# Second SwiGLU of a hybrid decoder layer: a fourth Strassen piece in the down products, with weight sums of two pieces made early and kept in DRAM

## The chip, the cores and the metric

The kernel runs on one core of a Trainium2 chip. The core has a matrix engine (TensorE, "PE" in the profile; its weight loads are listed apart as "PEld"), three engines for element-wise work (VectorE "DVE", ScalarE "ACT", GpSimd "POOL") and a synchronisation engine ("SP") that here only issues DMA transfers. Data lives in DRAM, in the on-chip memory SBUF, and, for results of TensorE, in eight PSUM banks. The metric is the time of one execution on the device in microseconds (us).

## The reference

One decoder layer for 256 positions of 1024 channels in float32. Three sub-layers follow each other, each between two RMS norms and added to the stream `h`. The first and the last are SwiGLUs with 2816 inner channels, the middle one is a mixer (a state-space branch and a differential attention, merged by gates).

```python
def rmsnorm(x, g):
    y = xf * lax.rsqrt(jnp.mean(xf * xf, axis=-1, keepdims=True) + EPS)
    return y.astype(x.dtype) * g

def swiglu(x, w_gate, w_up, w_down):
    return (jax.nn.silu(x @ w_gate) * (x @ w_up)) @ w_down
...
h = h + 0.5 * rmsnorm(swiglu(rmsnorm(h, ffn1_pre_g[l]), ffn1_w_gate[l], ffn1_w_up[l], ffn1_w_down[l]),
                      ffn1_post_g[l])
u = rmsnorm(h, mix_pre_g[l])
...
h = h + rmsnorm(merged @ w_out[l], mix_post_g[l])
h = h + 0.5 * rmsnorm(swiglu(rmsnorm(h, ffn2_pre_g[l]), ffn2_w_gate[l], ffn2_w_up[l], ffn2_w_down[l]),
                      ffn2_post_g[l])
```

The last SwiGLU is called f2 here, the first f1.

## The kernel before

**Splits.** A float32 product is made of three matmuls in the type fp32r. Each operand is split in a high half, which ScalarE makes by a cast, and a low half, which VectorE makes by subtracting the high half from the source. The three terms are high x high, low x high and high x low. For weights the halves are called `whi` and `wlo` (L271, L272), for the products of gate and up `gh` and `gl` (L332, L333).

**Weights.** All weights come in chunks of 1 MB, listed in `chunks` in the order of their use. `load_to` (L244) issues the loads on SP's queue, three raw buffers deep (`RAW_BUFS`). `split_steps` (L256) splits a chunk in two rows of 128x1024 on each engine, and `split_to` (L300) keeps the splits three chunks ahead of the matmuls. The halves live in a pool `k4` of 29 buffers of 4 KB a partition, which also holds the activations. When both halves of a chunk are made, its raw buffer is given to the next chunk.

**Gate and up.** The inner channels are cut into 11 pieces of T = 256. Pieces 0 and 1 are made first, by `pn_f` products with the positions on the partitions: the result is transposed (L978) and split from the PSUM tile `pt_f`. For pieces 2 to 10 `ffn` (L957) loops over `j`: gate chunk (`pg_f`), ScalarE's Silu, up chunk (`pup_f`), VectorE's product `sg` (L997), split into `gh` and `gl`. In the bank of a gate or up result the high and the low terms lie apart; ScalarE copies one (L359) and VectorE adds the other (L360), giving `sg` and `su`.

**Down.** The plan is a string, `DOWN` (L49), for both SwiGLUs "q1 p q2 p q3 ppp". A `p` is one piece of T: 24 matmuls of 128x512 and one weight chunk, so two low halves. A `qN` is a Strassen piece over pieces 2N and 2N+1: seven products p1 to p7 in place of eight, 42 matmuls in place of 48. Its operands are, beside quarters of the weights, four sums of quarters, made by VectorE (`wt`, L123) from the two raw chunks just before they are used, and four sums of the activations, made in `sums_of` (L743) while gate and up still run. Each of the seven weight operands is split by `Quad.split`: ScalarE `wqh` (L131), VectorE `wql` (L137). The products are taken in the order `FIRST` = 1, 2, 3, 5, 7, 6, 4, in the last Strassen piece in the order `LAST` = 1, 6, 7, 2, 3, 5, 4.

`mm_quads` (L834) takes the Strassen pieces and the plain ones between them, all added up in eight PSUM banks (L844), and `combine` (L869 to L872) puts the Strassen banks together. `mm_n` (L664, matmuls at L688) adds the remaining plain pieces and ends in the norm.

**Order.** Through most of f2 the order of the rows on each engine is set by the framework's scheduler, which works with its own costs and with the pools; each engine then executes its rows strictly in that order. A row that waits holds up all rows behind it on its engine. In the names below a number behind a tile's name is a counter: `wlo1050` is the low half 0 of chunk 105, `wql1145` the low half of product p5 of the Strassen piece that starts with chunk 114. In f2 chunks 93 to 110 are gate and up of pieces 2 to 10, in turns, and the down weights begin with chunk 111.

The functions that the change touches, with the loop over gate and up in `ffn`, follow.

## Time and profile before

| | |
|---|---|
| time, median of 3 runs | 728.9 us (728.49 to 729.12) |
| the profiled execution's own time | 728.89 us |
| its span | 727.2 us |
| TensorE busy | 719.8 us (99%), 4019 instructions |
| VectorE busy | 621.1 us (85%), 950 instructions |
| ScalarE busy | 478.8 us (66%), 816 instructions |
| GpSimd busy | 31.3 us (4%), 63 instructions |
| DMA | 137.93 MB, mean 190 GB/s |

The span goes from the first to the last recorded instruction; the profiled execution's time is 1.7 us longer. On the span's clock, f2's first products (`pn_f`) run from 541 to 564.6 us, gate and up from 564.6 to 665.2, the 174 matmuls of `mm_quads` from 665.2 to 704.6, the plain pieces behind them to 719.7; then come the last matmuls, the norm and the store.

How to read it: "L353 PE" is TensorE's work from line 353 of the kernel. A group's line gives busy time and mean duration, and behind them the engine's idle time ahead of its rows with the instruction that ended it ("<-ACT whi" means a cast on ScalarE was waited for). In lists of an engine's rows in time the first two columns are start and length in us. In a table of stretches the columns are the stretch, its length, and the busy times of PE, PEld, DVE, ACT and POOL, each with the number of rows, then the granted clock, the share of DMA time and the rate in GB/s. VectorE's rows overlap a little: a row of 128x1024 shows 1.22 us, and the next begins before it ends.

### The profile page before, as it was taken

The page shows a single profiled execution, that of the slowest core. Times are in us where ns is not written, and L with a number is a line of the kernel's source. Part 1 is how long each engine was busy: PE and PEld are TensorE (multiplying, and loading weights), DVE is VectorE, ACT ScalarE, POOL GpSimd, SP SyncE. Part 2 cuts the span into 40 slices and gives each one's busy share as a digit, 9 for nine tenths or more (in the row PEclk, how much of TensorE's full clock was granted, in tenths as well). Part 3 has the DMA queues.
Part 4 walks back from the last instruction along what each step waited for, and adds up shares of the span by engine and source line. Part 5 has one row for each costly group of instructions (what it writes and reads, how often), then busy time and mean ns, then how long its engine had stood idle before and what let it go on. Part 6 is the DMA issues. An engine that isn't in the chain of part 4 may idle for free.

```text
span 727.2 us, 10595 instructions
## 1 busy us (share of the span) xinstructions
PE 719.8 (99%) x4019; PEld 619.7 (85%) x4019; DVE 621.1 (85%) x950; ACT 478.8 (66%) x816; POOL 31.3 (4%) x63
## 2 busy tenths in 40 slices
PE   9999999999999999999999999999999999999996
PEld 8888888888878889999888788888888888888885
DVE  6978788999979999777996998789786878789996
ACT  5657566666867676969975577774664757576562
POOL 4300000000200000000000000000011000000000
PEclk9999999999999999999999999999999999999999
DMA  8874655567673557666564663474543654654551
GB/s 299 235 267 148 222 162 185 174 229 260 185 232 118 181 167 225 202 200 215 150 224 150 203 222 132 165 234 169 169 153 116 232 189 161 230 196 152 181 195 58
DMA packets 94452, 137.93 MB, mean 190 GB/s; under 512 B 2669, under 2 KB 68801, under 8 KB 94401
## 3 DMA queue, kind: packets, MB, share of 16 engines
q1 hardware_dynamic: 91728, 129.51, 54.4%
q0 software_dynamic: 2368, 7.22, 3.4%
q8 instruction: 31, 0.51, 0.3%
q10 hardware_dynamic: 304, 0.53, 0.2%
q14 instruction: 21, 0.16, 0.1%
HBM read 136.17 MB, written 1.08 MB: 189 GB/s over the span
## 4 chain that ended last, share of the span: by engine, by line
PE 91%; DVE 4%; ACT 2%; issue 1%; DMA 1%; DVEq 0%; ACTq 0%
PE pup_f L353 14%; PE pg_f L353 14%; PE pxs L353 6%; PE pws L394 6%; PE pgt L394 6%; PE acc_f2p L844 5%; PE pbc L353 3%; PE pk L353 3%; PE pq L353 3%; PE pwd L394 3%; PE pn_f L410 3%; PE pn_f L394 3%; PE acc_f1p L844 3%; PE pn_mx L394 2%; PE acc_f2p L688 2%; PE pz L345 2%
## 5 line engine op out<-in xcount | busy, mean ns | idle before, releaser
L272 DVE TENSOR_TENSOR wlo<-raw,whi 128x1024 fp32r<-128x1024 f32 x212 | 252.2, 1219 | 18.3 <-ACT whi L271 17.9
L271 ACT CAST whi<-raw 128x1024 fp32r<-128x1024 f32 x212 | 214.1, 1048 | 14.1 <-DMA raw<-in_w_in_dram 5.6
L353 PE MATMUL pg_f<-u_f,whi 128*128 128x512 f32 x288 | 69.0, 390 | 0.0
L353 PE MATMUL pup_f<-u_f,whi 128*128 128x512 f32 x288 | 68.7, 391 | 0.0
L353 PEld LDWEIGHTS pg_f<-u_f,whi 128*128 128x128 f32 x288 | 53.9, 188 | 11.1
L353 PEld LDWEIGHTS pup_f<-u_f,whi 128*128 128x128 f32 x288 | 52.9, 188 | 10.2
L131 ACT CAST wqh<-wt 128x1024 fp32r<-128x1024 f32 x24 | 25.2, 1054 | 23.2 <-DVE wt L123 22.0
L353 PEld LDWEIGHTS pg_f<-u_f,wlo 128*128 128x128 f32 x288 | 36.9, 191 | 1.4
L353 PE MATMUL pup_f<-u_f,wlo 128*128 128x256 f32 x288 | 37.5, 283 | 0.0
L353 PE MATMUL pg_f<-u_f,wlo 128*128 128x256 f32 x288 | 37.4, 283 | 0.0
L359 ACT COPY su_f<-pup_f 128x256 f32<-128x256 f32 x36 | 13.2, 373 | 35.9 <-PE pup_f L353 35.9
L353 PEld LDWEIGHTS pup_f<-u_f,wlo 128*128 128x128 f32 x288 | 35.9, 192 | 0.0
L360 DVE TENSOR_TENSOR su_f<-pup_f,su_f 128x256 f32<-128x256 f32 x36 | 15.2, 422 | 24.0 <-ACT su_f L359 23.9
L394 PE MATMUL pgt<-whi,u_mx 128*128 128x512 f32 x128 | 33.1, 393 | 0.0
L343 PE MATMUL pz<-u_mx,whi 128*128 128x256 f32 x128 | 31.6, 284 | 0.0
L342 PE MATMUL pz<-u_mx,whi 128*128 128x256 f32 x128 | 31.6, 284 | 0.0
L353 PE MATMUL pxs<-u_mx,whi 128*128 128x512 f32 x128 | 29.9, 390 | 0.0
L137 DVE TENSOR_TENSOR wql<-wt,wqh 128x1024 fp32r<-128x1024 f32 x24 | 29.1, 1219 | 0.2
L137 DVE TENSOR_TENSOR wql<-raw,wqh 128x1024 fp32r<-128x1024 f32 x21 | 25.4, 1219 | 3.4 <-ACT wqh L131 3.4
L394 PEld LDWEIGHTS pgt<-whi,u_mx 128*128 128x128 f32 x128 | 23.6, 188 | 5.3 <-issue 0.7
L353 PEld LDWEIGHTS pxs<-u_mx,whi 128*128 128x128 f32 x128 | 23.8, 188 | 4.8
L332 ACT CAST gh_f<-sg_f 128x512 fp32r<-128x512 f32 x18 | 11.2, 620 | 23.2 <-DVE sg_f L997 20.3
(487 smaller groups left out, 1607.7 us busy)
## 6 DMA issues: line engine op xcount, KB each, us to landing
raw<-in_w_in_dram SPq DMA_DIRECT2D x40, 1024.0 KB, 5.2
raw<-in_ffn_w_down_dram SPq DMA_DIRECT2D x22, 1024.0 KB, 4.9
raw<-in_ffn_w_gate_dram SPq DMA_DIRECT2D x20, 1024.0 KB, 5.4
raw<-in_ffn_w_up_dram SPq DMA_DIRECT2D x20, 1024.0 KB, 5.2
raw<-in_ssd_w_branch_dram SPq DMA_DIRECT2D x8, 1024.0 KB, 5.0
acb<-acd POOLq DMA_DIRECT2D x8, 512.0 KB, 4.7
raw<-in_da_w_branch_dram SPq DMA_DIRECT2D x4, 1024.0 KB, 5.8
raw<-in_w_out_dram SPq DMA_DIRECT2D x4, 1024.0 KB, 4.9
```

Source lines behind the costliest of these rows:

```text
L131: nc.scalar.copy(hi, src)
L137: nc.vector.tensor_sub(lo, src, hi.bitcast(F32))
L271: last_cast[0] = behind(nc.scalar.copy(hi, r[:, js, :]), "cast").ins
L272: m = nc.vector.tensor_sub(lo, r[:, js, :], hi.bitcast(F32))
L342: nc.tensor.matmul(acc[m], wh(j)[:, cs], ah(k0 + j), start=first and j == ks[0], stop=False)
L343: nc.tensor.matmul(acc[m], wh(j)[:, cs], al(k0 + j), start=False, stop=False)
L345: nc.tensor.matmul(acc[m], wl(j)[:, cs], ah(k0 + j), start=False, stop=last and j == ks[-1])
L353: nc.tensor.matmul(to, w_(j)[:, m * P:(m + 1) * P], x_(j), start=first and j == 0, stop=not first and j == KD - 1, skip_group_check=True)
L360: nc.vector.tensor_tensor(dst, acc[:, :T], dst, ALU.add)
L394: nc.tensor.matmul(acc, a(k0 + j), b(j), start=first and i == 0, stop=last and i == 11)
L410: nc.tensor.matmul(accs[b], x_(k0 + j), w_(j), start=first and j == 0 and w_ is wh and x_ is acts[b][0], stop=last and j == 3 and w_ is wl)
L844: nc.tensor.matmul(bank[p], x_, w_, start=p not in begun, stop=last and p in (1, 5, 6, 7))
```

## The change

- f2's plan becomes "q1 Q2 q3 Q0 ppp": the two plain pieces between the Strassen pieces (pieces 0 and 1) become a fourth Strassen piece, 0, which is now the last one and has the order `LAST`. f1's plan stays.
- `Q` is a Strassen piece with stored sums (class `Stored`). While gate and up run, `stored_sums` loads the four quarters of the piece's weights (`ws`) on GpSimd's queue into four buffers of `k4`, makes the four sums on VectorE in the same buffers, and stores each to a DRAM tile `sums_f2...` on GpSimd's queue. `ffn` steps it at fixed pieces `j`: first the job of Q2, then that of Q0. In the down products the sums come back as chunks like others, on SP's queue, so that `Stored.split` has no sums to make. For Q2 and Q0 together the down products now load eight chunks: per piece half a chunk for p1, one for p2 and p3, and two with sums.
- The chunks with sums go into the pool `u8`, whose two buffers hold the normed activations until gate and up have read them. `refill` replaces the plain call of `load_to` where a raw buffer is given back, and keeps the two kinds of buffer apart; `opened` lets the sums' loads begin only when `mm_quads` is built.
- The activations of pieces 0 and 1 are needed unsplit for piece 0's sums, so ScalarE also copies `pt_f` (`first`, two rows of 128x512), and `sums_of(0)` runs at the end of the loop's first turn. In `sums_of`, groups 0 and 3 take one split of 128x1024 in buffers of `k4` where there were one of 128x768 in `k3` and one of 128x256; this touches f1's and the mixer's too.
- `begin` in `mm_n` becomes a list of the banks not begun before it.

```diff
-DOWN = {"f1": "q1 p q2 p q3 ppp", "f2": "q1 p q2 p q3 ppp"}
+DOWN = {"f1": "q1 p q2 p q3 ppp", "f2": "q1 Q2 q3 Q0 ppp"}
...
-                    load_to(self.i + j + 1 + RAW_BUFS)
+                    refill()
...
+    class Stored(Quad):
+        def __init__(self, i, products, at):
+            self.i, self.products, self.at = i, products, at
+            self.uses = [[p for p in products if at[p][0] == n] for n in range(4)]
+        def split(self, p):
+            n, part = self.at[p]
+            load_to(self.i + n + 1)
+            src = part(raws[self.i + n])
+            hi, lo = (k4([P, 2, 512], f"wq{x_}{self.i}{p}", F32R) for x_ in "hl")
+            nc.scalar.copy(hi, src)
+            nc.vector.tensor_sub(lo, src, hi.bitcast(F32))
+            self.uses[n].remove(p)
+            if not self.uses[n]:
+                raws[self.i + n] = None
+                refill()
+            return lambda kt: hi[:, kt, :], lambda kt: lo[:, kt, :]
...
+    def stored_quad(w, k0, products, tag):
+
+        n, first = len(units), len(chunks)
+        sums = products[1:3] + products[5:] if products[1] == 6 else products[3:]
+        store = dram.tile([P, 4, D], F32, name=f"sums_{tag}{k0}")
...
+            if p == 1:
+                chunk(w[k0:k0 + 2 * P, :512].rearrange("(j p) c -> p j c", p=P), [P, 2, 512])
+                at[1] = (i, lambda r: r)
+            elif p == 2:
+                n_chunk(w, k0 + 2 * P)
+                at[2], at[3] = (i, lambda r: r[:, :, :512]), (i, lambda r: r[:, :, 512:])
+            else:
+                j = sums.index(p)
+                homes[len(chunks)] = tag
+                chunk(store[:, j:j + 2, :], [P, 2, D])
+                for o in range(2):
+                    at[sums[j + o]] = (i, lambda r, o=o: r[:, o, :].rearrange("p (k c) -> p k c", k=2))
+        del units[n:]
+        q = Stored(first, products, at)
+        units.extend((q, p) for p in products)
+        return w, k0, sums, store
...
+    def stored_sums(w, k0, sums, store):
+        t = [k4([P, 2, 512], f"ws{k0}{n}") for n in range(4)]
+        for n in (1, 0, 3, 2):
+            rows = w[k0 + n // 2 * 2 * P:k0 + (n // 2 + 1) * 2 * P, n % 2 * 512:(n % 2 + 1) * 512]
+            nc.gpsimd.dma_start(t[n], rows.rearrange("(k p) c -> p k c", p=P))
+        yield
+        for p, n, a, b in ((5, 0, 1, 0), (7, 1, 3, 1), (6, 3, 3, 0), (4, 2, 2, 3)):
+            nc.vector.tensor_sub(t[n], t[a], t[b])
+            nc.gpsimd.dma_start(store[:, sums.index(p), :], t[n].rearrange("p k c -> p (k c)"))
+            yield
...
+            elif kind == "Q":
+                stored.setdefault(tag, []).append(stored_quad(wd[0], j * 2 * T, products, tag))
...
+    def refill():
+        while len(raws) < len(chunks):
+            at_home = lambda i: (homes.get(i) is None) == (homes.get(len(raws)) is None)
+            if sum(r is not None and at_home(i) for i, r in enumerate(raws)) >= (2 if len(raws) in homes else RAW_BUFS):
+                break
+            if len(raws) in homes and homes[len(raws)] not in opened:
+                break
+            load_to(len(raws) + 1)
...
+            if i in homes:
+                if homes[i] not in opened:
+                    return
+                r = sb.tile([P, 4, 2, T], F32, tag="u8", name=f"raw{i}", bufs=2)
+                r = r.rearrange("p (a b) c t -> p a (b c t)", a=2)
+            else:
+                r = sb.tile(shape, F32, tag="raw", name=f"raw{i}", bufs=RAW_BUFS)
...
+                                             (b, q) in begin and i == 0 and kt == 0 and x_ is ah and w_ is wh,
...
+        full = g in (0, 3)
+        hi, lo = ((k4 if full else k3)([P, 4 if full else 3, 2, P], f"s{n}{g}", F32R) for n in "hl")
+        more = None if full else k2([P, 2, 2, P], f"s4{g}", F32R)
...
+        if full:
+            split(hi, lo, v)
+            return tuple([x_[:, i] for i in range(4)] for x_ in (hi, lo))
...
+        opened.add(tag)
+        refill()
...
+            if 0 in QUADS[tag]:
+                nc.scalar.copy(first[0][:, :, bs], pt_)
...
+        first = [k4([P, 4, T], f"g0_{tag}")] if 0 in QUADS[tag] else []
...
+        jobs = [stored_sums(*job) for job in stored.get(tag, ())]
+        def store_sums(at):
+            for i in at:
+                if i < len(jobs):
+                    next(jobs[i])
...
+            store_sums({4: (0,), 6: (0,), 8: (1,)}.get(j, ()))
...
+            if first:
+                sums[0] = sums_of(0, first[0][:, :2, :], first[0][:, 2:, :])
+                del first[0]
+            store_sums({2: (0,), 4: (0, 0), 5: (1,), 6: (1, 1), 8: (1,)}.get(j, ()))
```

The matmuls in `mm_quads` are 168 in place of 174; in the new kernel their line is L927. On GpSimd's queue 16 transfers stand where there was none: four loads, four stores, twice.

**Gate and up, VectorE.** Before, around the product of piece 6 (`sg_f26` by `su_f26`):

```order
L272 TENSOR_TENSOR wlo1040_6209<-raw104_6050,whi1040_6208 128x1024
L272 TENSOR_TENSOR wlo1041_6213<-raw104_6050,whi1041_6212 128x1024
L360 TENSOR_TENSOR su_f26_6207<-pup_f260_6218,su_f26_6207 128x256
L360 TENSOR_TENSOR su_f26_6207<-pup_f261_6219,su_f26_6207 128x256
L997 TENSOR_TENSOR sg_f26_6157<-su_f26_6207,sg_f26_6157 128x512
L333 TENSOR_TENSOR gl_f26_6156<-sg_f26_6157,gh_f26_6155 128x512
L272 TENSOR_TENSOR wlo1050_6261<-raw105_6100,whi1050_6260 128x1024
L272 TENSOR_TENSOR wlo1051_6265<-raw105_6100,whi1051_6264 128x1024
L272 TENSOR_TENSOR wlo1060_6311<-raw106_6166,whi1060_6310 128x1024
L360 TENSOR_TENSOR sg_f27_6259<-pg_f270_6270,sg_f27_6259 128x256
L360 TENSOR_TENSOR sg_f27_6259<-pg_f271_6271,sg_f27_6259 128x256
L272 TENSOR_TENSOR wlo1061_6315<-raw106_6166,whi1061_6314 128x1024
```

Now, at the same product; `ws0n` are the quarters, and then the sums, of Strassen piece 0:

```order
L437 TENSOR_TENSOR su_f26_6239<-pup_f260_6250,su_f26_6239 128x256
L349 TENSOR_TENSOR wlo1040_6241<-raw104_6072,whi1040_6240 128x1024
L349 TENSOR_TENSOR wlo1041_6245<-raw104_6072,whi1041_6244 128x1024
L437 TENSOR_TENSOR su_f26_6239<-pup_f261_6251,su_f26_6239 128x256
L222 TENSOR_TENSOR ws01_6178<-ws03_6180,ws01_6178 128x1024
L1093 TENSOR_TENSOR sg_f26_6187<-su_f26_6239,sg_f26_6187 128x512
L437 TENSOR_TENSOR sg_f27_6295<-pg_f270_6306,sg_f27_6295 128x256
L437 TENSOR_TENSOR sg_f27_6295<-pg_f271_6307,sg_f27_6295 128x256
L410 TENSOR_TENSOR gl_f26_6186<-sg_f26_6187,gh_f26_6185 128x512
L222 TENSOR_TENSOR ws03_6180<-ws03_6180,ws00_6177 128x1024
L349 TENSOR_TENSOR wlo1050_6297<-raw105_6122,whi1050_6296 128x1024
L349 TENSOR_TENSOR wlo1051_6301<-raw105_6122,whi1051_6300 128x1024
```

Two sums (rows of L222) stand among the rows of piece 6, the gate's additions of piece 7 (`sg_f27`) come before the low halves of chunk 105, and `gl_f26` no longer stands right behind the product.

**Gate and up, ScalarE.** Before, around the casts of the last gate chunk (109):

```order
L271 CAST whi1080_6426<-raw108_6268 128x1024
L271 CAST whi1081_6430<-raw108_6268 128x1024
L427 ACTIVATE sg_f28_6375<-sg_f28_6375 128x512
L359 COPY su_f28_6425<-pup_f280_6436 128x256
L359 COPY su_f28_6425<-pup_f281_6437 128x256
L332 CAST gh_f28_6373<-sg_f28_6375 128x512
L271 CAST whi1090_6478<-raw109_6318 128x1024
L271 CAST whi1091_6482<-raw109_6318 128x1024
L271 CAST whi1100_6528<-raw110_6384 128x1024
L359 COPY sg_f29_6477<-pg_f290_6488 128x256
L359 COPY sg_f29_6477<-pg_f291_6489 128x256
L271 CAST whi1101_6532<-raw110_6384 128x1024
```

Now:

```order
L436 COPY su_f28_6460<-pup_f280_6471 128x256
L348 CAST whi1070_6409<-raw107_6248 128x1024
L348 CAST whi1071_6413<-raw107_6248 128x1024
L436 COPY su_f28_6460<-pup_f281_6472 128x256
L348 CAST whi1080_6461<-raw108_6304 128x1024
L348 CAST whi1081_6465<-raw108_6304 128x1024
L436 COPY sg_f29_6514<-pg_f290_6525 128x256
L436 COPY sg_f29_6514<-pg_f291_6526 128x256
L409 CAST gh_f28_6406<-sg_f28_6408 128x512
L504 ACTIVATE sg_f29_6514<-sg_f29_6514 128x512
L348 CAST whi1090_6515<-raw109_6354 128x1024
L348 CAST whi1091_6519<-raw109_6354 128x1024
```

The casts of chunk 107 and 108 have moved back, behind the first copy of `su_f28`; those of chunk 109 stand behind the copies of the gate bank of piece 9 (`sg_f29`) and its Silu, where they stood ahead of them.

**Down products, TensorE.** Before, at the products p5 and p7 of Strassen piece 2 (`sh2`, `sl2` are its activation sums):

```order
L844 MATMUL acc_f2p5_6716<-wqh1145_6754,sh2_6144 128x512
L844 MATMUL acc_f2p5_6716<-wqh1145_6754,sl2_6145 128x512
L844 MATMUL acc_f2p5_6716<-wql1145_6758,sh2_6144 128x512
L844 MATMUL acc_f2p5_6716<-wqh1145_6754,sh2_6144 128x512
L844 MATMUL acc_f2p5_6716<-wqh1145_6754,sl2_6145 128x512
L844 MATMUL acc_f2p5_6716<-wql1145_6758,sh2_6144 128x512
L844 MATMUL acc_f2p7_6721<-wqh1147_6768,sh2_6144 128x512
L844 MATMUL acc_f2p7_6721<-wqh1147_6768,sl2_6145 128x512
L844 MATMUL acc_f2p7_6721<-wql1147_6772,sh2_6144 128x512
L844 MATMUL acc_f2p7_6721<-wqh1147_6768,sh2_6144 128x512
```

Now, at p5 and p7 of Strassen piece 3, which follows Q2 directly:

```order
L927 MATMUL acc_f2p5_6745<-wqh1175_6837,sh3_6398 128x512
L927 MATMUL acc_f2p5_6745<-wqh1175_6837,sl3_6399 128x512
L927 MATMUL acc_f2p7_6750<-wqh1177_6853,sh3_6398 128x512
L927 MATMUL acc_f2p5_6745<-wql1175_6841,sh3_6398 128x512
L927 MATMUL acc_f2p5_6745<-wqh1175_6837,sh3_6398 128x512
L927 MATMUL acc_f2p5_6745<-wqh1175_6837,sl3_6399 128x512
L927 MATMUL acc_f2p5_6745<-wql1175_6841,sh3_6398 128x512
L927 MATMUL acc_f2p7_6750<-wqh1177_6853,sl3_6399 128x512
L927 MATMUL acc_f2p6_6749<-wqh1176_6865,sh3_6398 128x512
L927 MATMUL acc_f2p7_6750<-wql1177_6857,sh3_6398 128x512
L927 MATMUL acc_f2p7_6750<-wqh1177_6853,sh3_6398 128x512
L927 MATMUL acc_f2p7_6750<-wqh1177_6853,sl3_6399 128x512
```

Before, p5's six matmuls were all ahead of p7's, as in the code; in the new kernel, at this piece, p7's first row stands between p5's second and third, and a matmul of p6 between p7's.

**Down products, SP.** Before, the loads of the last nine chunks:

```order
L253 DMA raw113_6536<-in_ffn2_w_down_dram 128x2x1024
L253 DMA raw114_6602<-in_ffn2_w_down_dram 128x2x1024
L253 DMA raw115_6656<-in_ffn2_w_down_dram 128x2x1024
L253 DMA raw116_6670<-in_ffn2_w_down_dram 128x2x1024
L253 DMA raw117_6760<-in_ffn2_w_down_dram 128x2x1024
L253 DMA raw118_6786<-in_ffn2_w_down_dram 128x2x1024
L253 DMA raw119_6812<-in_ffn2_w_down_dram 128x2x1024
L253 DMA raw120_6858<-in_ffn2_w_down_dram 128x2x1024
L253 DMA raw121_6892<-in_ffn2_w_down_dram 128x2x1024
```

Now the loads from the first half chunk of Q2 to the end of Q0:

```order
L330 DMA raw113_6573<-in_ffn2_w_down_dram 128x2x512
L330 DMA raw115_6751<-sums_f21024_66 128x2048
L330 DMA raw114_6639<-in_ffn2_w_down_dram 128x2x1024
L330 DMA raw116_6753<-sums_f21024_66 128x2048
L330 DMA raw117_6755<-in_ffn2_w_down_dram 128x2x1024
L330 DMA raw118_6757<-in_ffn2_w_down_dram 128x2x1024
L330 DMA raw119_6767<-in_ffn2_w_down_dram 128x2x512
L330 DMA raw120_6777<-sums_f20_67 128x2048
L330 DMA raw122_6845<-sums_f20_67 128x2048
L330 DMA raw121_6843<-in_ffn2_w_down_dram 128x2x1024
```

The first sums of Q2 (chunk 115) are loaded ahead of its chunk 114, and in Q0 the second sums (122) ahead of chunk 121.

More of the change, by code (lines that the diff above doesn't have):

```diff
@@ L877, in combine @@
             add(c4, bank[5], u3)
-        return acc, [[p1, u4], [u3, c4]], combine, [j for kind, j in down[tag][n_quads:]]
+        return acc, [[p1, u4], [u3, c4]], combine, [j for kind, j in down[tag][n_quads:]], \
+            [(b, q) for b in range(2) for q in range(2) if ((2, 3), (4, 8))[b][q] not in begun]
     class Norm:
@@ L1025, in done @@
             ready(b)
[L1027 removed]
+        mm_n(acc, gu, done, turned, pairs=pairs, begin=begin,
              taken_all=combine, norms=norms, half=half, quarters=quarters, tail=tail)
```

26 lines of the change are left out of this document (12 added, 14 removed).

## The prediction

> **What bounds the kernel now.** I read the page's shares first, then TensorE's waits, then the chain in order of time through the second SwiGLU, and only then the engine that feeds it.
>
> ```profile
> PE 719.8 (99%) x4019; PEld 619.7 (85%) x4019; DVE 621.1 (85%) x950; ACT 478.8 (66%) x816; POOL 31.3 (4%) x63
> ...
> PE 91%; DVE 4%; ACT 2%; issue 1%; DMA 1%; DVEq 0%; ACTq 0%
> ```
> ```profile
> PE warm L487 <- DVE zeros L467: 1.1, 1, 1.1
> ```
> ```profile
> 659.77 5.57 PE pup_f L353 x32
> 665.34 39.44 PE acc_f2p L844 x174
> 704.78 14.96 PE acc_f2p L688 x66
> 719.74 0.73 PE tail L688 x6
> ```
> TensorE waits for nobody but once at the start (1.1 us). In the down products 174 matmuls follow each other in 39.44 us, 0.2267 us apiece. So any matmul removed there is worth 0.2267 us, and no stall is left for the change to remove. But VectorE, which makes the low halves of the weights, is nearly full:
>
> ```profile
> 586.20:651.60 65.40, 65.40 (x380) 57.98 (x380) 52.23 (x77) 41.91 (x66) 0.00 (x0) 1.00 0.57 187
> 651.60:665.30 13.70, 13.70 (x77) 12.00 (x76) 12.27 (x16) 8.49 (x12) 0.00 (x0) 1.00 0.53 194
> 665.30:704.60 39.30, 39.30 (x175) 32.54 (x174) 38.06 (x36) 25.13 (x29) 0.63 (x1) 1.00 0.59 195
> ```
> The columns are length, then busy time of PE, PEld, DVE, ACT, POOL, clock, DMA share, GB/s. In the first stretch, most of gate and up, VectorE has 13.17 us idle in 65.40; in the down products 1.24 us in 39.30. How early it is there shows in when the low half of the last product of each Strassen piece is ready, against the matmul that reads it:
>
> ```profile
> 667.44 1.21 DVE L137 TENSOR_TENSOR wql<-wt,wqh 128x1024 fp32r<-128x1024 f32 x1
> ...
> 672.75 0.69 DVE L333 TENSOR_TENSOR gl_f<-sg_f,gh_f 128x512 fp32r<-128x512 f32 x1 [0.76 <-ACT gh_f L332]
> ...
> 683.92 2.49 DVE L137 TENSOR_TENSOR wql<-wt,wqh 128x1024 fp32r<-128x1024 f32 x2
> ...
> 699.13 2.35 DVE L137 TENSOR_TENSOR wql<-wt,wqh 128x1024 fp32r<-128x1024 f32 x2
> 701.40 6.89 DVE L272 TENSOR_TENSOR wlo<-raw,whi 128x1024 fp32r<-128x1024 f32 x6
> ```
> ```profile
> 665.18 0.39 PE L844 MATMUL acc_f2p<-wqh,gh_f 128*128 128x512 f32 x1
> ...
> 673.79 0.39 PE L844 MATMUL acc_f2p<-wql,gh_f 128*128 128x512 f32 x1
> ...
> 688.75 0.39 PE L844 MATMUL acc_f2p<-wql,gh_f 128*128 128x512 f32 x1
> ...
> 703.71 0.39 PE L844 MATMUL acc_f2p<-wql,gh_f 128*128 128x512 f32 x1
> ```
> Ready at 668.65, 686.41, 701.48; read at 673.79, 688.75, 703.71. The lead falls from 5.1 to 2.3 and 2.2 us. That lead is the cover the change draws on.
>
> **The change part by part.** *Removed.* Two plain pieces of 24 matmuls become one Strassen piece of 42: six matmuls less, 6 x 0.2267 = 1.36 us off TensorE (the diff's pieces and the built order give the same count). This is all it can gain.
>
> *Moved in VectorE's down work.* A Strassen piece needs 11 wide instructions (4 sums, 7 low halves), a piece with stored sums 7, a plain one 2. Six in a row take 6.89 us, so one costs (6.89 - 1.22)/5 = 1.13 us, 1.22 being the mean of the rows below. Per piece VectorE needs 12.4 (q), 7.9 (Q) or 2.3 us (p); TensorE 9.52, 9.52 and 5.44. Before, q1 p q2 loses 2.9, gains 3.1, loses 2.9: 2.7 behind at its worst. Now q1 Q2 q3 loses 2.9, gains 1.6, loses 2.9: 4.2 behind at the end of q3. So q3 is where the lead is tested.
>
> *Added in gate and up, VectorE.*
>
> ```profile
> L272 DVE TENSOR_TENSOR wlo<-raw,whi 128x1024 fp32r<-128x1024 f32 x24 | 28.5, 1218 | 0.8 <-ACT whi L271 0.8
> L360 DVE TENSOR_TENSOR su_f<-pup_f,su_f 128x256 f32<-128x256 f32 x12 | 5.1, 422 | 10.7 <-ACT su_f L359 10.7
> ...
> L333 DVE TENSOR_TENSOR gl_f<-sg_f,gh_f 128x512 fp32r<-128x512 f32 x6 | 4.1, 688 | 2.2 <-ACT gh_f L332 2.2
> ```
> ```profile
> 579.66 3.50 DVE L272 TENSOR_TENSOR wlo<-raw,whi 128x1024 fp32r<-128x1024 f32 x3 [0.26 <-ACT whi L271]
> 583.08 0.75 DVE L360 TENSOR_TENSOR sg_f<-pg_f,sg_f 128x256 f32<-128x256 f32 x2
> 583.74 1.21 DVE L272 TENSOR_TENSOR wlo<-raw,whi 128x1024 fp32r<-128x1024 f32 x1
> ```
> Between the `su` addition at 586.2 and the second half of the last up chunk (651.6), the new order has 8 sums more, and four of the low halves above (579.66 x3, 583.74) now stand behind it, where they were ahead: 12 x 1.13 = 13.6 us into 13.17 us of idle time. With no wait left the stretch would end at 586.2 + 52.2 + 13.6 = 652.0; with all old waits at 665.2. I take 657.0, nearer the first: the 10.7 us before `su` are waits for TensorE's own pace, which vanish when VectorE comes 1.2 us late; the 2.2 us before `gl_f` go too, since in the new order other rows stand between the product and `gl_f`. What I leave, 5.0 us, comes from walking the new order with these durations: ScalarE now copies the next gate bank (`sg_f29`) and applies Silu before it casts the last gate chunk's weights (`whi109`), so VectorE waits there some 1 us, 1.4 us at the fourth piece's sums, and 0.3 to 0.6 at some places more.
>
> *From there to the end of q3*: 29 wide rows (11 + 7 + 11) x 1.13 = 32.8, three `su` and two `sg` additions 1.7, two products and two `gl_f` 2.4, two waits of 0.76 for `gl_f`'s cast, as at 672.75, and two of 0.4 for the cast that follows it on ScalarE (1.05 less the 0.62 that `gl_f` hides): 39.2 us. So the last low half of q3 is ready at 657.0 + 39.2 = 696.2. It is the 123rd matmul of the down products that reads it, at 665.2 + 122 x 0.2267 = 692.9. TensorE loses 3.3 us at q3 and none later: Q0 takes VectorE 7.9 of TensorE's 9.52 us. Net +3.3 - 1.4 = +1.9 us, here taken as 2.0.
>
> *Added on ScalarE.* Two copies of 128x512 (0.59 in the first row below) and three more casts (1.05 in the second): it is busy 41.91 of 65.40 and 25.13 of 39.30, so nothing; without that cover 4.3 us. Sums of quad 0's activations: four short VectorE rows and one wide, 2.5 us, into the 4.5 us that the four low halves leave before 586.2: nothing.
>
> ```profile
> 696.66 0.59 ACT L872 COPY p_f<-acc_f2p 128x512 f32<-128x512 f32 x1 [0.21 <-PE acc_f2p L844]
> ```
> ```profile
> L271 ACT CAST whi<-raw 128x1024 fp32r<-128x1024 f32 x212 | 214.1, 1048 | 14.1 <-DMA raw<-in_w_in_dram 5.6
> ...
> L359 ACT COPY su_f<-pup_f 128x256 f32<-128x256 f32 x36 | 13.2, 373 | 35.9 <-PE pup_f L353 35.9
> ```
> *Added transfers.* Eight loads and eight stores of 512 KB on POOL's queue; and eight chunks (7 MB) in place of four (4 MB) for the two pieces.
>
> ```profile
> acb<-acd POOLq DMA_DIRECT2D x8, 512.0 KB, 4.7
> ...
> out_dram<-h SPq DMA_DIRECT2D x2, 256.0 KB, 2.1
> ```
> ```profile
> DMA to landing us min/median/max: 3.4/5.2/9.2
> ```
> No 512 KB store is in the trace: between 2.1 us and the 9.2 of the slowest megabyte, 4.7 by the nearest. Second job: its loads can start when gate matmuls of the fifth piece free the buffers, about 600, and VectorE first needs them at about 617; hidden even at 9.2. Stores: the nearest reader of their buffers comes 14 us later; hidden. The stored sums wait for the normed activations' buffers, free about 664.4; in SP's order the plain chunk of Q2 stands behind the first sums, so it lands between 664.4 + 3.4 (the two side by side) and 664.4 + 2 x 5.2 = 674.8 (one after the other); ScalarE, behind VectorE, reaches it at about 675. Hidden, by little at that end; beyond it each late us is a late us at q3.
>
> A rule speaks against the POOL queue. Row first:
>
> ```profile
> L1350 POOL DMA_DIRECT2D acb<-acd x8: 527/530/572, 277.4 to 346.3; - x8
> ...
> 277.40:350.00 72.60, 72.50 (x597) 68.18 (x596) 59.27 (x97) 57.79 (x109) 4.28 (x8) 1.00 0.66 206
> ```
> With VectorE busy 59.27 of 72.60 us, eight such issues took 0.53 us each and landed in 4.7. The Trainium skill's "SBUF — State Buffer", section "Summary: rules for kernel authors", says that a DMA issued by GpSimd should not be hidden under VectorE work in a 2x or 4x mode, as its descriptors are starved. By that warning the time would be the third rival's 732.9. Its section "Who interferes with whom" reports that two-input tensor operations did not stall such DMAs; nearly all of VectorE's rows here are of that kind, the trace agrees, and by this it stays at 730.9.
>
> The sum: 728.9 (profiled run 728.89: span 727.2 plus 1.7 around it; the median of the three runs is 728.9 too) + 2.0 = 730.9.
>
> **The rivals.**
> - *The cover holds* (other side). VectorE ends the gate/up stretch by 657.0 - 3.3 = 653.7: then q3 waits for nothing and the time is 728.9 - 1.4 = 727.5. Break-even is 655.1. For it: 13.17 us idle against 13.6 added. Against it: the built order interleaves the products of q3, p7 between p5, as a scheduler does that finds the operands late; the old order never does.
> - *Gate and up stall too.* Nothing there stalls now, but the order puts ScalarE's copy of an up bank (`su_f28`) ahead of the next gate chunk's cast (`whi107`): copy 0.37 and cast 1.05 against some 1.6 us until the matmuls want it. If 0.6 us goes lost at each of nine pairs, 5.4 us, TensorE is late by more than q3's stall, which it replaces: 728.9 + 5.4 - 1.4 = 732.9, and up to 735 if VectorE shifts too.
> - *POOL's transfers are late*, VectorE stands at a sum that has not landed, and all low halves behind it wait. With five times the issue time, 2.65 us, four issues and 4.7 us of landing end at 615.3: just in time; a further 2 us of lateness goes to q3 whole: 732.9.
> - *The sums come late to the down products* (the stored sums do not do their work): if the two loads ran one after the other at 9.2 us each, Q2's plain chunk would land at 682.8, 7.8 us after ScalarE wants it; half of that makes 730.9 + 3.9 = 734.8. It decides from 675 on. Against it: 9.2 is the one slowest landing of the whole run, 5.2 the median.
>
> **How the numbers follow.** Changes below 0.2% (1.5 us) are about what a measurement here cannot tell from none. Forecast 0.62, its own range 729.2 to 733.0 (VectorE 2 us either way), two thirds of it above 730.4. Cover holds 0.18. Gate and up stall 0.12. POOL late 0.04. Sums late 0.04. The gain is at most 1.36 us, 0.19%, so faster by over 0.2% needs luck: 0.03. Same: 0.15 from the cover, 0.20 from the forecast's lower third: 0.35. Slower: 0.42 + 0.20 = 0.62. The range is 727.3 to 735.0: from the full gain to the last stalls.
>
> **What would show it.** Down products: TensorE's chain has 168 matmuls (L927 of the changed kernel) instead of 174, with gaps under wqh and wql of q3 (its p5, p7, p6, p4), released by ACT L131 and DVE L137, some 3 us in sum, and none in Q0. VectorE's idle time from 586 to 657 falls from 13 to about 5 us and its last up chunk ends near 657. The POOL loads show no waiter. Wrong if VectorE ends that chunk before 654, if gaps stand at its L430 (gate and up), or if its L156 (the casts of stored sums) waits for a DMA.

## The result, and the profile after

The changed kernel takes 733.3 us (median of 4 runs, 732.24 to 734.85) against 729.0 us for the kernel before: a ratio of 1.0061, 95% interval 1.0041 to 1.0080. It is some 4.3 us slower. The profiled execution took 733.49 us, with a span of 731.8 us, 4.6 us more than before.

The page's shares, and its chain that ended last:

```profile
PE 720.5 (98%) x4013; PEld 617.3 (84%) x4013; DVE 630.3 (86%) x959; ACT 482.4 (66%) x819; POOL 42.0 (6%) x79
...
PE 82%; DVE 8%; ACT 4%; DMA 3%; issue 2%; DVEq 0%; ACTq 0%
```

Before, 91% of the chain was TensorE; now VectorE, ScalarE and transfers hold 15%. What TensorE waits for (us in total, times, longest us):

```profile
PE acc_f2p L927 <- ACT wqh L131: 1.4, 3, 0.6
PE pg_f L430 <- ACT whi L348: 1.2, 1, 1.2
PE warm L564 <- DVE zeros L544: 1.1, 1, 1.1
PE acc_f2p L765 <- DVE wlo L349: 0.5, 1, 0.5
...
PE acc_f2p L927 <- ACT wqh L156: 0.2, 1, 0.2
```

Only the third line was there before. The places, in TensorE's rows in time:

```profile
583.68 3.81 PE L430 MATMUL pup_f<-u_f,whi 128*128 128x512 f32 x16
588.67 3.93 PE L430 MATMUL pg_f<-u_f,whi 128*128 128x512 f32 x16 [1.18 <-ACT whi L348]
...
666.86 0.39 PE L927 MATMUL acc_f2p<-wqh,gh_f 128*128 128x512 f32 x1
...
678.80 0.51 PE L927 MATMUL acc_f2p<-wqh,s 128*128 128x512 f32 x1 [0.21 <-ACT wqh L156]
...
691.61 0.50 PE L927 MATMUL acc_f2p<-wqh,sh 128*128 128x512 f32 x1 [0.15 <-ACT wqh L131]
...
692.87 0.39 PE L927 MATMUL acc_f2p<-wqh,sl 128*128 128x512 f32 x1
693.87 0.50 PE L927 MATMUL acc_f2p<-wqh,sh 128*128 128x512 f32 x1 [0.61 <-ACT wqh L131]
...
696.14 0.51 PE L927 MATMUL acc_f2p<-wqh,gh_f 128*128 128x512 f32 x1 [0.61 <-ACT wqh L131]
```

A wait costs more than its bracket shows: from 692.87 to 693.87 there is 1.00 us where 0.2267 would do, a loss of 0.77, of which 0.61 is named. Reckoned so, from start to start, TensorE loses 1.68 us in gate and up (the down products start at 666.86 in place of 665.18), 0.86 around the start of Q2, 2.27 in q3 at its last products, and 0.86 at the last plain chunk. That is 5.67; less the 1.36 of the six matmuls, 4.31 us. The rest of the 4.6 us of span is spread in the tail and in smaller steps.

VectorE in the stretches that the prediction looked at:

```profile
586.20:657.00 70.80, 69.62 (x396) 61.03 (x395) 65.15 (x92) 46.53 (x73) 7.30 (x12) 1.00 0.78 268
...
666.90:708.00 41.10, 39.51 (x169) 31.04 (x168) 40.03 (x40) 29.97 (x33) 0.54 (x1) 1.00 0.83 301
```

It has 5.65 us idle in the first and 1.1 us in the second. The last low half of the last up chunk ends at 656.59 + 1.22 = 657.8:

```profile
656.59 1.22 DVE L349 TENSOR_TENSOR wlo<-raw,whi 128x1024 fp32r<-128x1024 f32 x1
```

The forecast had put this at 657.0. But the chain, followed back from the gap at 588.67, shows two things that the forecast did not have. A load of an up chunk, issued at 567.11, stands in it with 8.93 us (the median was 5.2 before). And behind it, from 582.27 to 586.08, stand the sums of piece 0's activations (VectorE's `sv` and `sl`, ScalarE's `sh`), 3.8 us that the forecast had put at nothing:

```profile
567.11 8.93 DMA raw<-in_ffn_w_up_dram
...
576.06 1.06 ACT whi L348
577.12 0.02 issue
577.14 2.36 DVE wlo L349 x2
...
582.27 0.34 DVE sv L828
...
583.77 1.06 ACT sh L409
...
584.86 1.23 DVE sl L410
...
587.32 0.35 ACT su_f L436
587.67 0.95 ACT whi L348
588.63 0.04 issue
588.67 5.84 PE pg_f L430 x32
```

ScalarE stood 4.58 us for that chunk in the changed kernel; in the kernel before, where the cast is L271, it stood 0.64 us for the same one. ScalarE's rows in time, first after, then before:

```profile
576.06 2.00 ACT L348 CAST whi<-raw 128x1024 fp32r<-128x1024 f32 x2 [4.58 <-DMA raw<-in_ffn_w_up_dram]
```
```profile
571.91 2.00 ACT L271 CAST whi<-raw 128x1024 fp32r<-128x1024 f32 x2 [0.64 <-DMA raw<-in_ffn_w_up_dram]
```

The first job's four loads had been issued just ahead of it on GpSimd's queue:

```profile
561.90 0.82 POOL L219 DMA_DIRECT2D ws<-in_ffn_w_down_dram  x1 [13.38 <-PE pn_f L471]
563.73 2.19 POOL L219 DMA_DIRECT2D ws<-in_ffn_w_down_dram  x3 [1.01 <-PE pn_f L471]
```

In the table of stretches (busy us and instructions of TensorE, its weight loads, VectorE, ScalarE and GpSimd, then the granted clock, the DMA share and GB/s) the 16 DMA engines are full from 567 to 576 us, a share of 1.00 at 350 GB/s. Before, in the second fence, it was 0.93 at 305:

```profile
567.00:576.00 9.00, 9.00 (x57) 8.04 (x56) 5.98 (x8) 4.41 (x7) 0.00 (x0) 1.00 1.00 350
```
```profile
567.00:576.00 9.00, 9.00 (x56) 8.11 (x55) 8.20 (x10) 6.53 (x10) 0.00 (x0) 1.00 0.93 305
```

### The profile page after: what moved, and what is told of

The parts are those of the page before. It is cut to its first block, busy times and chain, and to the rows that moved or that the text cites. A ratio compares the mean times of both kernels' runs of the same rounds, so it can differ in the third digit from the quotient of the medians.

```text
span 731.8 us, 10659 instructions
## 1 busy us (share of the span) xinstructions
PE 720.5 (98%) x4013; PEld 617.3 (84%) x4013; DVE 630.3 (86%) x959; ACT 482.4 (66%) x819; POOL 42.0 (6%) x79
## 4 chain that ended last, share of the span: by engine, by line
PE 82%; DVE 8%; ACT 4%; DMA 3%; issue 2%; DVEq 0%; ACTq 0%
PE pg_f L430 12%; PE pup_f L430 12%; PE pxs L430 6%; PE pws L471 6%; PE pgt L471 6%; PE pbc L430 3%; PE pk L430 3%; PE pq L430 3%; PE pn_f L487 3%; PE pwd L471 3%; PE pn_f L471 3%; PE acc_f2p L927 3%; PE pn_mx L471 2%; DVE wlo L349 2%; DVE wt L123 2%
## 5 line engine op out<-in xcount | busy, mean ns | idle before, releaser
L349 DVE TENSOR_TENSOR wlo<-raw,whi 128x1024 fp32r<-128x1024 f32 x208 | 247.9, 1220 | 24.4 <-ACT whi L348 23.8
L348 ACT CAST whi<-raw 128x1024 fp32r<-128x1024 f32 x208 | 210.1, 1048 | 19.2 <-DMA raw<-in_w_in_dram 5.3
L430 PE MATMUL pg_f<-u_f,whi 128*128 128x512 f32 x288 | 69.5, 391 | 1.2 <-ACT whi L348 1.2
L430 PE MATMUL pup_f<-u_f,whi 128*128 128x512 f32 x288 | 68.7, 391 | 0.0
L430 PEld LDWEIGHTS pg_f<-u_f,whi 128*128 128x128 f32 x288 | 53.8, 188 | 12.9 <-ACT whi L348 1.6
L430 PEld LDWEIGHTS pup_f<-u_f,whi 128*128 128x128 f32 x288 | 52.9, 188 | 10.2
L430 PEld LDWEIGHTS pg_f<-u_f,wlo 128*128 128x128 f32 x288 | 37.0, 191 | 1.5
L430 PE MATMUL pg_f<-u_f,wlo 128*128 128x256 f32 x288 | 37.5, 282 | 0.0
L430 PE MATMUL pup_f<-u_f,wlo 128*128 128x256 f32 x288 | 37.5, 283 | 0.0
L430 PEld LDWEIGHTS pup_f<-u_f,wlo 128*128 128x128 f32 x288 | 35.9, 192 | 0.0
L131 ACT CAST wqh<-wt 128x1024 fp32r<-128x1024 f32 x20 | 21.1, 1053 | 20.2 <-DVE wt L123 19.0
L430 PE MATMUL pxs<-u_mx,whi 128*128 128x512 f32 x128 | 29.9, 390 | 0.0
L430 PEld LDWEIGHTS pxs<-u_mx,whi 128*128 128x128 f32 x128 | 23.8, 188 | 4.8
L420 PEld LDWEIGHTS pz<-u_mx,whi 128*128 128x128 f32 x128 | 24.5, 192 | 0.2 <-issue 0.2
L419 PEld LDWEIGHTS pz<-u_mx,whi 128*128 128x128 f32 x128 | 24.5, 192 | 0.0
```

The source lines that it names most:

```text
L131: nc.scalar.copy(hi, src)
L348: last_cast[0] = behind(nc.scalar.copy(hi, r[:, js, :]), "cast").ins
L349: m = nc.vector.tensor_sub(lo, r[:, js, :], hi.bitcast(F32))
L419: nc.tensor.matmul(acc[m], wh(j)[:, cs], ah(k0 + j), start=first and j == ks[0], stop=False)
L420: nc.tensor.matmul(acc[m], wh(j)[:, cs], al(k0 + j), start=False, stop=False)
L430: nc.tensor.matmul(to, w_(j)[:, m * P:(m + 1) * P], x_(j), start=first and j == 0, stop=not first and j == KD - 1, skip_group_check=True)
```

## The experiments

Theory 1 is the forecast's: VectorE's added work makes it late for the down products. Theory 2 was formed from the trace above: the loads of the quarters slow the chunk beside them, and the lateness starts there. All ratios are to the kernel before, run on the same chip. An edit can also move the scheduler's order of the rows, so a run may change more than its edit says.

**The old plan with the side changes.**

```diff
-"f2": "q1 Q2 q3 Q0 ppp"
+"f2": "q1 p q2 p q3 ppp"
```

> The changed kernel with f2's plan put back to q1 p q2 p q3 ppp, so that of the change only the side changes stay (refill, one wide split in sums_of for groups 0 and 3 of f1 and the mixer, the list begin). If the whole cost lies in f2's new plan and its transfers, this runs as the kernel before: 728.5 to 729.5 us. Rival: the side changes in f1 and the mixer cost something; then over 730.5 us, with the loss ahead of 541 us.

Measured 728.55 us, ratio 1.0001 (0.9992 to 1.0010). The side changes cost nothing; all of the loss belongs to f2's plan and what comes with it.

**Short sums.**

```diff
-nc.vector.tensor_sub(t[n], t[a], t[b])
+nc.vector.tensor_sub(t[n][:, :, 0:8], t[a][:, :, 0:8], t[b][:, :, 0:8])
```

> The eight weight sums in gate and up are made on 16 of their 1024 columns only (the rest of the stored tiles keeps the raw quarters, so the products of Q2 and Q0 are not the reference's); loads, stores and plan stay. It takes some 8 x 1.0 us off VectorE. Theory 1 (VectorE's added work makes it late for the down products): the gaps ahead of Q2 (0.8 us) and in q3 (2.2 us) go, the loss in gate and up (1.8 us) and the wait for the last plain chunk (0.8 us) stay: 733.3 - 3.0 = 730.3 us. Rival (the gaps come from the order of the rows or from the transfers): 732.5 us or more.

Measured 728.88 us, ratio 1.0007 (0.9998 to 1.0016). All waits in the down products went, that for the last plain chunk too, which I had expected to stay. What stays beside the start-up is the gap in gate and up, with the same chunk late (8.79 us in the chain):

```profile
PE warm L564 <- DVE zeros L544: 1.1, 1, 1.1
PE pg_f L430 <- ACT whi L348: 1.0, 1, 1.0
```

So the waits in the down products need VectorE's sums of the weights; the gap at 588 us does not.

**Short loads.**

```diff
-nc.gpsimd.dma_start(t[n], rows.rearrange(...))
+nc.gpsimd.dma_start(t[n][:, :, 0:64], rows.rearrange(...)[:, :, 0:64])
...
-nc.vector.tensor_sub(t[n], t[a], t[b])
+nc.vector.tensor_sub(t[n], *(quarters of uT, the normed activations))
```

> The loads of the weight quarters bring 64 of 512 columns only, and the eight sums, full size, are made of the normed activations in place of the quarters (so the stored sums are not the reference's); plan, sums, stores stay. Theory 2 (the first four loads slow the up chunk that is loaded beside them, 8.9 us in place of 5.2, and ScalarE, VectorE and the gate matmuls at 587 us wait for it): that chunk lands in about 5.2 us, the loss of 1.8 us in gate and up goes: 731.5 us, and down to 729.5 if VectorE's lateness at q3 came from there too. Rival (the wait at 587 us comes from VectorE's work and the order alone): 733 us with the wait still there.

Measured 727.48 us, ratio 0.9989 (0.9980 to 0.9998): faster than the kernel before. TensorE waits for nothing but the start-up, with all eight sums at full size. VectorE ends gate and up at 651.84, as early as before the change (651.69):

```profile
649.49 2.35 DVE L349 TENSOR_TENSOR wlo<-raw,whi 128x1024 fp32r<-128x1024 f32 x2
```

So the eight sums do fit into VectorE's idle time in this order of rows, and the waits in the down products do not come without the loads. The table of stretches shows one place where the two meet: from 564.5 to 587 us VectorE does 19.49 us of work here and 16.22 in the changed kernel, which waits 4.07 us there behind the late chunk. Those 3.3 us are pushed into the stretches that the sums have filled.

```profile
564.50:587.00 22.50, 22.50 (x132) 19.88 (x131) 19.49 (x28) 14.86 (x23) 1.44 (x3) 1.00 0.64 218
```
```profile
564.50:587.00 22.50, 22.50 (x133) 19.90 (x132) 16.22 (x23) 11.54 (x19) 1.42 (x2) 1.00 0.80 272
```

The first row is of the short loads, the second of the changed kernel. But the loads' size is not all that differs. The order has changed as well, and the last of the eight sums stands some 12 us earlier here (first row) than in the changed kernel (second):

```profile
625.91 1.22 DVE L222 TENSOR_TENSOR ws<-u_f 128x1024 f32<-128x1024 f32 x1
```
```profile
638.27 1.22 DVE L222 TENSOR_TENSOR ws<-ws,ws 128x1024 f32<-128x1024 f32 x1
```

So this run does not part the loads' own effect from that of the order that comes with them.

**Loads alone.** The eight loads in the old plan, without sums, stores or stored pieces (`stored` gets two jobs for f2, and the loop of sums is empty).

> The changed kernel's eight loads of weight quarters alone: f2's plan is q1 p q2 p q3 ppp again, nothing is summed or stored, and nobody reads what is loaded. The first four start at the same place, about 562 us, so the up chunk issued at 567 us should land in some 8.9 us again and ScalarE wait 4 to 4.6 us for it. In this kernel's order ScalarE casts the first weights of piece 4 (whi97) ahead of both copies of su_f23, as in the kernel before, while the changed kernel has one copy ahead of them. If the loads cost time only where that order and VectorE's added work have used up the cover: no wait at 587 us, none in the down products, 728.5 us. Rival (the late chunk costs by itself): 730 us with the wait at 587 us, or more.

Measured 728.73 us, ratio 1.0002 (0.9993 to 1.0012); TensorE waits for nothing. The loads went out earlier than in the changed kernel (the first of them 7.5 us ahead of the up chunk's load, in place of 5.2), and ScalarE waited 2.47 us for the up chunk, less than expected; it waited 3.29 more at 606 us, behind the second job's loads:

```profile
573.22 2.00 ACT L348 CAST whi<-raw 128x1024 fp32r<-128x1024 f32 x2 [2.47 <-DMA raw<-in_ffn_w_up_dram]
606.42 1.05 ACT L348 CAST whi<-raw 128x1024 fp32r<-128x1024 f32 x1 [3.29 <-DMA raw<-in_ffn_w_up_dram]
```

Both disappear in idle time. So in the old plan the loads cost nothing. In the new plan sums without loads cost nothing (727.48, the short loads), loads with hardly any sums cost 1.4 us (728.88 for the short sums, less 727.48), and both together cost 5.3 us (4.3 above the kernel before in the changed kernel, 1.0 below it with the short loads). The two parts are not additive, though part of this may be the order of rows.

**Four Strassen pieces without stored sums.**

```diff
-"f2": "q1 Q2 q3 Q0 ppp"
+"f2": "q1 q2 q3 q0 ppp"
```

> Four Strassen pieces without stored sums: plan q1 q2 q3 q0 ppp. No added loads, stores or sums in gate and up. By the forecast's balance VectorE needs 12.4 us a piece and TensorE 9.5; before, VectorE was 5.1 us ahead at the end of q1, so three more pieces of 2.9 us leave TensorE waiting 3.6 us: 728.9 - 1.4 + 3.6 = 731.1 us. If the stored sums relieve the down products by more than they cost elsewhere, this is slower than the changed kernel's 733.3 us instead.

Measured 738.19 us, ratio 1.0135 (1.0121 to 1.0149). My estimate missed 7 us. From start to start TensorE loses 7.8 us in the Strassen pieces, where it had 3.6, and 2.7 at the plain pieces behind them, where it had nothing. It left out that piece 10's last addition, product and split stand on VectorE behind q1's last low half (669.73 to 672.57 us), 2.8 us; the other 4 us are not explained by a run. The waits are mostly for ScalarE's casts of sums that VectorE has just made:

```profile
PE acc_f2p L927 <- ACT wqh L131: 4.8, 6, 1.8
...
PE acc_f2p L765 <- ACT whi L348: 0.7, 1, 0.7
PE acc_f2p L765 <- DVE wlo L349: 0.7, 2, 0.5
```

So the stored sums do their work in the down products, worth 5.4 us even with the late up chunk (9.7 above the kernel before here, 4.3 in the changed kernel).

**Late loads and early loads.** Two ways to move the first job's loads away from 567 us.

```diff
-store_sums({2: (0,), 4: (0, 0), ...
+store_sums({3: (0,), 4: (0, 0), ...
```

> The changed kernel with the first job's four loads one piece later (behind piece 3 in place of piece 2); they can start when piece 2's up matmuls free their buffers, about 575 us in place of 562. Theory 2: the up chunk issued at 567 us lands in some 5 us, and its wait goes; the chunks issued from 575 us land later instead, and if these have more slack the time is 727.5 to 729.5 us. Rival (any 2 MB beside gate and up cost the same wherever they are): 733 us, with the same wait some pieces later.

Measured 730.45 us, ratio 1.0026 (1.0017 to 1.0036). The chunk is in time (ScalarE waits 0.85 us for it), the gap in gate and up is gone, the waits in the down products stay (2.8 us from start to start). VectorE ends gate and up at 654.8, 3 us earlier than the changed kernel's 657.8 and 3 us later than the short loads' 651.8. So the waits in the down products do not need the late chunk, against theory 2, which had 729.5 us at most. For the other way the first step of the job stands ahead of `products(evict, back)`:

> The changed kernel with the first job's four loads moved ahead of f2's first products (they are free to start near the end of the mixer, some 30 us earlier); sums, stores and the second job stay where they are. Theory 2 (contention of these loads with the up chunk loaded at 567 us): that chunk lands in some 5 us again, TensorE waits neither at 587 us nor in the down products: 727.5 us, as with the short loads. Rival (VectorE's added work alone fills its idle time, whatever the loads do): 731 us or more, with gaps at q3.

Measured 733.96 us, ratio 1.0078 (1.0066 to 1.0091). Nothing waits at 588 us or in the down products, as theory 2 said. But all four sums of the first job are made here before gate and up begin (the last starts at 560.88), so theory 1 would say the same of the down products. And gate and up begin 6.8 us late (571.42 in place of 564.62), for a reason in neither theory: a queue that stands still. The job now runs while the mixer ends. VectorE's first sum waits 3.99 us for its quarter, and the store of that sum waits on GpSimd's queue for VectorE. Behind it there stand the rows of the mixer's norm (L600), which ran at 542.26 in the changed kernel. So `h` is late, and with it ScalarE and the first products of f2. GpSimd's and ScalarE's rows:

```profile
546.48 0.59 POOL L223 DMA_DIRECT2D sums_f<-ws  x1 [5.94 <-DVE ws L222]
547.15 1.34 POOL L600 TENSOR_SCALAR rp_mxp<-sp_mxp 128x1 f32<-128x1 f32 x1
```
```profile
550.03 0.63 ACT L595 ACTIVATE sq_f<-h 128x512 f32<-128x512 f32 x1 [7.98 <-DVE h L734]
```

What early loads alone would give, with the store behind those rows, was not tried. The changed kernel has a queue like this too. The forecast let the second job's loads start at about 600 us; they went out at 609.39, behind the store of the first job's last sum, which waited for VectorE:

```profile
608.83 0.53 POOL L223 DMA_DIRECT2D sums_f<-ws  x1 [9.71 <-DVE ws L222]
609.39 2.90 POOL L219 DMA_DIRECT2D ws<-in_ffn_w_down_dram  x4
```

With the early loads, where that store is long done, they begin at 601.55, although gate and up run later.

**Loads on SP's queue.**

```diff
-nc.gpsimd.dma_start(t[n], rows.rearrange(...))
+nc.sync.dma_start(t[n], rows.rearrange(...))
```

> The changed kernel with the loads of the weight quarters on SP's queue in place of GpSimd's: in SP's order the first job's four stand behind the gate and up chunks of pieces 3 and 4 (the last of them issued at about 580 us) and ahead of a chunk that is issued at about 591 us anyway; the second job's four likewise stand between two chunks. Theory 2: the chunk issued at 567 us has the transfers for itself again and lands in some 5 us, VectorE's cover holds, and all waits go: 727.5 us. Rival (the first sum now waits for its quarters, which land at about 588 us when VectorE wants them, or a later chunk comes late behind them): 730 us or more.

Measured 732.13 us, ratio 1.0055 (1.0041 to 1.0068). The wait at 588 us went, and another came at 622.46 (1.41 us). There ScalarE's second copy of `su_f`, which waits 1.30 us for TensorE's bank, stands ahead of the cast of the next gate chunk: a like order to that at 588 us. That the loads have a part in this one is not shown. This run also gives no sign that GpSimd's way of issuing was the trouble. The time from issue to landing of a 512 KB quarter (least, median, most) was, in the changed kernel and with SP's queue:

```profile
DMA to landing us min/median/max: 4.4/7.2/8.5
```
```profile
DMA to landing us min/median/max: 6.9/7.6/8.4
```

**Sums on GpSimd.**

```diff
-nc.vector.tensor_sub(t[n], t[a], t[b])
+nc.gpsimd.tensor_sub(t[n], t[a], t[b])
```

> The changed kernel with the eight weight sums in gate and up made by GpSimd in place of VectorE. VectorE gets 8 x 1.13 = 9 us back, the loads stay. Theory 1 with theory 2: as with the short sums, the gaps in the down products go and the wait at 587 us (1.5 us) stays: 728.9 us. Rival: GpSimd's sums slow VectorE's rows beside them, or take so long that the stores come late: 731 us or more.

Measured 740.25 us, ratio 1.0157 (1.0144 to 1.0171): the rival. GpSimd takes about 2.5 us a sum, and VectorE's rows beside it stretch. In groups by line, from 570 to 590 us, first this kernel and then the changed one (count, busy us, mean ns):

```profile
L349 DVE TENSOR_TENSOR wlo<-raw,whi 128x1024 fp32r<-128x1024 f32 x5 | 10.0, 2039 | 2.1 <-ACT whi L348 2.0
```
```profile
L349 DVE TENSOR_TENSOR wlo<-raw,whi 128x1024 fp32r<-128x1024 f32 x6 | 7.2, 1220 | 4.2 <-ACT whi L348 4.1
```

This is what the Trainium skill's "SBUF — State Buffer", section "Who interferes with whom", states: a VectorE instruction with two inputs in SBUF and a GpSimd instruction that reads SBUF exclude each other. The runs agree.

**Later sums.** Three schedules with the first job's loads late, in search of a version below the kernel before. In the first the first job's sums are emitted later:

> The late loads (first job's loads behind piece 3) and also its sums later: one behind piece 4, two behind piece 5, in place of one in the middle of piece 4 and two behind it. With the late loads VectorE waited 2.75 us for the quarters ahead of its first sum, and TensorE 2.1 us in the down products. If that wait is what VectorE's lateness at Q2 and q3 came from, it goes, and the time is 727.5 to 728.5 us. Rival (the sums, later, meet the second job's and the end of gate and up): 730 us or more, as with the late loads.

Measured 730.43 us, ratio 1.0025 (1.0016 to 1.0034), unchanged. I had taken the wait for the first job's; it is for the second's, at 619 us, and it is still there:

```profile
619.33 1.23 DVE L222 TENSOR_TENSOR ws<-ws,ws 128x1024 f32<-128x1024 f32 x1 [2.53 <-DMA ws<-in_ffn_w_down_dram]
```

The other two emit the second job later (`6: (0, 1)` in the first table, and `3: (0,), 4: (0, 0), 6: (1, 1), 8: (1,)` or `3: (0,), 4: (0, 0), 6: (1,), 7: (1, 1), 8: (1,)` in the second):

> First job's loads behind piece 3 (as in the late loads), and the second job's loads emitted with piece 6, so that in VectorE's order its first sum stands some five rows later (behind the product of piece 6), where its quarters should have landed. With the late loads VectorE's last up chunk ended 10.2 us ahead of the down products and TensorE waited 2.1 us in Q2 and q3; with the short loads it ended 12.7 us ahead and nothing waited. If the 2.75 us for the second job's quarters are what is missing, the lead is 12.9 us here, nothing waits, and the time is 727.5 us, below the kernel before. Rival (the sums, later, only move the wait towards the down products): lead about 10 us, 730.4 us.

> As the run before, with the second job's loads and sums about one piece later still (loads behind piece 6, two sums behind piece 7, one behind 8). By the same theory the quarters have landed before VectorE wants them, and 727.5 to 728 us; but the last two sums now stand within some 15 us of the end of gate and up, so if the place of the sums counts, the lead is smaller than in the run before and the time 728.5 to 730.5 us.

Measured 729.94 us, ratio 1.0019 (1.0010 to 1.0027), and 730.70 us, 1.0031 (1.0020 to 1.0041). In both VectorE no longer waits for quarters. Yet its lead, the time from the end of the last up chunk's low half to the first down product, is only 10.6 and 8.3 us. Set side by side over the runs, with TensorE's loss in the 168 matmuls of the Strassen pieces (from the first one's start to that of the first plain matmul, less 168 x 0.2267):

| kernel | lead, us | loss in the Strassen pieces, us |
|---|---|---|
| short sums | 13.5 | 0 |
| early loads | 12.9 | 0 |
| short loads | 12.7 | 0 |
| sums on GpSimd | 12.1 | 0.9 |
| spread | 10.6 | 2.2 |
| loads on SP | 10.5 | 2.2 |
| late sums | 10.4 | 2.3 |
| late loads | 10.2 | 2.8 |
| changed kernel | 9.1 | 3.1 |
| spread more | 8.3 | 3.2 |

From a lead of some 12.5 us on, nothing waits. Below that the loss grows as the lead shrinks, from 0.9 us at 12.1 to 3.2 at 8.3. With short loads a first sum is already made at 583 us, in idle time, and the last at 626; with late loads the first stands at about 594 and the last at 636. With real loads in gate and up the sums fall later, into VectorE's full part. Whether that is for the loads' landing or for the order that the scheduler chose is not settled: in the changed kernel, and in the last two schedules, no sum waits for its quarters. I found no schedule with real loads that beats the kernel before.

## Why the prediction was right or wrong

- *Direction and size.* Forecast slower, 730.9; measured 733.3, inside the whole range, 0.3 us above the forecast's own range. The loss is 4.3 us where 2.0 was forecast, more than twice. What is over is for the most part the gap in gate and up (1.7) and the wait for the last plain chunk (0.9), which the sum did not have.
- *The gain of 1.36 us.* Nearly there: with short loads nothing is lost, and the medians show 1.0 us.
- *"I take 657.0, nearer the first."* This step failed, and that the number came out at 657.8 is luck. The 5.0 us that I left as waits of VectorE for ScalarE's new order did not come as reckoned: with short loads, in an order of its own, the stretch ends at 651.8, at the bound of "no wait left" (652.0). The real 6 us go with the loads. Some 3 of them go with the late up chunk, since the stretch ends at 654.8 where that chunk is in time (late loads); the other 3 go with the later place of the sums, and what sets that place is open.
- *The wait at q3 of 3.3 us.* The size was good: 2.3 in q3 and 0.9 at Q2, which I had not placed there. The count behind it (39.2 us of VectorE to the last low half of q3) holds: it ends 697.35, 39.5 us after 657.8. The lead that it asks for, 11.5 us, was some 1 us too small.
- *Gate and up.* I gave the stall 0.12, at nine pairs of 0.6 us. It came at one, for 1.7 us, and three things stand in its chain: the chunk late by the loads, the sums of piece 0's activations, and the order, which puts ScalarE's copy of `su_f23` ahead of the next gate chunk's cast (587.32 and 587.67 above). I had put those sums at nothing, into 4.5 us of cover; with short loads they cost nothing, but behind the late chunk the cover was gone. With the short sums of the weights the late chunk still makes the gap. With the loads alone there is none: the chunk was less late, that kernel has no sums of piece 0, and the cast stands ahead of both copies. Which of these differences spared it is open.
- *The rivals on transfers.* I asked only whether the new transfers would be in time for their own readers. They were: no row waits for a quarter in the changed kernel. What I did not ask is whom they delay. On the rule against GpSimd's queue, the measurement is for the other side: on SP's queue the quarters land no sooner. What the runs show is that the DMA engines together were full beside the late chunk, a share of 1.00 at 350 GB/s, and that the chunk is in time where the quarters are small or go out later. The Trainium skill's "DMA: Bandwidth & Descriptors", section "Specifications", gives about 358 GB/s from HBM as the limit for a core. The trace does not bear that out as a limit: from 671 to 680 us the changed kernel moves 414 GB/s at a share of 1.02.
- *The wait for the last plain chunk* (0.9 us) was in no term. It goes with VectorE's lateness, as the short sums show: that chunk's load waits for a buffer that a low half of Q0 gives back.
- *What would be wrong.* I named gaps at L430 as a sign against me, and there is one. ScalarE's L156 did not wait for a transfer; at Q2 it stood behind the cast of `gh_f`, which waited 2.80 us for VectorE's product.

## What to carry to other kernels

A transfer that is added beside tight loads has to be asked two things: whether it lands in time for its reader, and which load already in flight lands later for it. Look for the stretch where the DMA share is near 1 and for the load there with the shortest slack. Idle time of an engine is one purse: added work and an added wait may each fit alone and not together, so the two have to be summed over the same stretch before either is called hidden. And a step that is moved earlier takes its waits with it: what stands behind its store on the same queue waits too.

## What was not expected of the hardware

A matmul that has waited is followed by some that run slower: after each gap in the down products the next start comes some 0.34 us later in place of 0.2267, so that the wait of 0.61 us at 693.87 cost 0.88 in all. GpSimd's sums made VectorE's low halves beside them take 2.04 us in place of 1.22 on average; there TensorE waits 6.2 us at two gate chunks and 2.4 at an up chunk. The other one is of the queues: a store that waited for its sum held back GpSimd's own rows, which had nothing to do with it, by 4.9 us (547.15 against 542.26, early loads).
